# Transposing branch B's probabilities by DMA in 16-bit halves, with the attention steps at new slots

## The chip, the cores and the metric

The kernel runs on one core of one Trainium2 chip. Its time is what the device takes for one execution, in microseconds (us), and a version is timed in several runs, of which the median counts. The engines are named as in the profile: PE (TensorE, with PEld for its weight loads), DVE (VectorE), ACT (ScalarE), POOL (GpSimd) and SP (SyncE, which issues most DMA transfers). Each works through a queue of its own in order and meets the others only at semaphores.

## The reference

It is one decoder layer on 512 tokens of width 2048. One projection of the normed input feeds three token mixers; their outputs are gated, projected, weighted and summed. The change lies in branch B, the "forgetting attention" of 12 heads of width 64:

```python
def forgetting_attention(q, k, v, f_logit, q_gain, k_gain):
    ...
    c = jnp.cumsum(log_f, axis=1).transpose(0, 2, 1)
    ...
        sc = jnp.einsum('bqhd,bshd->bhqs', qb, k) * scale + cqb[..., None] - c[:, :, None, :]
        qpos = n * BLOCK + jnp.arange(BLOCK)
        mask = key_pos[None, :] <= qpos[:, None]
        sc = jnp.where(mask[None, None], sc, NEG)
        p = jax.nn.softmax(sc, axis=-1)
        return jnp.einsum('bhqs,bshd->bqhd', p, v)
```

Branch A is a sliding-window attention, also of 12 heads, and branch C a cross-attention of 4 heads into 256 memory tokens. All of it is float32.

## The kernel before

**Matmuls.** A float32 operand is split into a high and a low part (tensors with `h`/`hi` and `l`/`lo`, or weight tiles `wb` and `wc`), and each product is made of three matmuls. The weights come as a stream of units (`Stream`): a unit is 256 rows of one projection, four banks by two row blocks by three matmuls, 24 in all, each 128x384 or wider. For each unit SP fetches a raw tile `wa` (two buffers), ACT casts it to the high part `wb` in two casts (L212), and DVE subtracts for the low part `wc` (L215). When unit i begins, the casts of unit i+1 are recorded and the fetch of unit i+2.

**Slots.** The order of the work is fixed while the program is written down. A clock counts slots: three projection matmuls are half a slot, so a unit is four slots. `at_slot` and `later` put a step at a slot, and the tables at the top of the file say how far a step stands from its base. PE, DVE, ACT and POOL execute exactly in the order of recording; for SP's queue a scheduler chooses the order. Attention is thus woven into the projections: branch B's first six heads (0 to 5) run beside the projections of the second half of branch B, heads 6 to 11 beside those of branch A, branch A's heads beside the next, and so on. Slots are counted in this text from the first unit; branch B's attention stands between slots 96 and 288.

**One head of branch B** (`head_B`) is a chain of steps, and a step waits in the chain when a resource such as a PSUM bank ("T") or a buffer is not free in the program. `sb` makes a bias tile on POOL. `s1(i)`, for the four query blocks i, multiplies queries and keys (PE, tile `sB`), adds the bias and takes the maximum (DVE, L600), and later exponentiates (ACT, L603) and divides (DVE, L580 and L581), leaving the probabilities in `p` (`pB`), one row per query. `s2` transposes them on PE against an identity into PSUM (`ptB`, L625), ten blocks of 128x128 in three groups, and `split` casts each group to the high part `phB` (ACT, L556) and subtracts for the low part `plB` (DVE, L558). `s3` multiplies both with V (`avB`, L635, eight matmuls), and `pv_out` copies half of the result (`avsB`) and adds.

`prep` stands ahead of every second head: four transposes each of the queries (`tqB`) and of the keys (`tkB`), from which ACT makes two query copies (L538) and four key copies (L549, L552) and DVE the low parts (L539, L550).

A later stage of the kernel already has a transpose by DMA: `flip_dma` separates the two 16-bit halves of float32 values on ACT, sends them through `dma_start_transpose` in tiles of 128 partitions by 2048 halves, and ACT joins the halves again (L1478).

Of the kernel before, what the change touches and what calls it, by code (L numbers as in the profile page):

```python
# [20 lines left out]
P = 128  # L21
# [10 lines left out]
UK = 2  # L32
BOFF = (0, 512, 1024, 896)

BASES_B = ((14, 24, 35.5, 46, 52, 70.5), (15, 24, 34.5, 47, 58, 72.5))
# [6 lines left out]
PREP_Q = ((-1.5, 22.0, 38.5), (2.5, 18.5, 45.5))  # L42
PREP_K = ((6.5, 28.0, 44), (7, 26.5, 53.5))
PREP_A = (6, 18.5, 39.0, 46, 66.0, 76.5)
PREP_KA = (6.0, 32.5, 47.5, 68.0)

NORMS = {'qB0': (24.5, 3, 2), 'kB0': (10.5, 4.5, 4.5), 'qB1': (3.5, 3, 1.0), 'kB1': (1.5, 7.0, 1), 'qA0': (6, 2.5, 3.5), 'qA1': (6.0, 3.0, 1.5), 'kA': (0.5, 3, 0.0), 'mk': (8.0, 4.0, 0.0), 'qC0': (0.5, 3, 0), 'qC1': (4.5, 2.5, 1.5)}


LOW_W, LOW_M, LOW_Q, LOW_K, LOW_P = ((1.0, 1), (0.5, 1.5), 1, 1, 0.5)  # L50
EXP_B, EXP_A, EXP_C, DIV_B, DIV_A, DIV_C = (1.0, 0.5, 1.0, 3, 3.5, 3.0)
PV_B, PV_A = ((1.0, 3.5), (0.5, 1))
SUMS_X = (1, 13, 23, 133, 112, 207, 190, 225)

# [3 lines left out]
def tile_hybrid_block(ctx, tc, xT, x, memT, mem, ng, mng, w_in, b_forget, gqa, gka, sinks, gqb, gkb, gqc, gkc,  # L58
# [10 lines left out]
    def f32(ap):  # L69
        return ap.bitcast(F32)  # L70
# [72 lines left out]
    def later(dt, f):  # L143
        at_slot(clock[0] + dt, f)
# [11 lines left out]
            heapq.heappop(agenda)[2]()  # L156

    chains, chain_end = [], [0.0]
    free = {"T": 2, "P": 2, "PT": 1, "Q": 3, "KH": 3, "KL": 2, "bias": 2, "cb": 2}

    def release(*names):
        for n in names:
# [225 lines left out]
        at_slot(t0 + 24, lambda: root(ss, mrstd, 2))  # L388


    def qk_tile(name, tag, n, bufs):
        return tokp.tile([P, NT, n], F32, tag=tag, bufs=bufs, name=name)

# [29 lines left out]
    def evac_qk(key, tag, n, hd, bufs, scale=rstd, nt=NT, after=None):  # L423

        nh = n // hd
        state = {}

        def f(b, pb, c0=0):
            if after is not None:
                after(b, pb)  # L430
            if b == 0:
                state["t"] = tokp.tile([P, nt, n], F32, tag=tag, bufs=bufs, name=f"t_{key}")
            t = state["t"]
            if scale is None:
                ac.copy(t[:, b, :], pb[:, c0:c0 + n])
            else:
                ac.activation(t[:, b, :], pb[:, c0:c0 + n], AF.Copy, scale=scale[:, b:b + 1])
# [81 lines left out]
    def tbank(name):  # L519
        return bank(0, name)  # L520
# [62 lines left out]
    def head_B(h, kv):  # L583
# [3 lines left out]
        def s1(i):  # L587
# [14 lines left out]
            release("bias")  # L602
            later(EXP_B, lambda: ac.activation(pi, pi, AF.Exp, bias=nm, scale=-1.0, accum_out=den[:, i:i + 1]))  # L603
            later(DIV_B, lambda: scaled(pi, den, i, ve))

        def sb(i):
            n = (i + 1) * P
# [3 lines left out]
                             fill=NEG, base=0, channel_multiplier=1)  # L611
            s["b", i] = bi

        def s2(g):
            p = s["p"]
            if g == 0:
                s["hi"] = at.p.tile([P, 1280], F32R, tag="PH", bufs=1, name=f"phB{h}")
                s["lo"] = at.p.tile([P, 1280], F32R, tag="PL", bufs=1, name=f"plB{h}")
            off = (0, 128, 384, 768)
            grp, o, n = (((0,), 0, 512), ((1, 3), 512, 512), ((2,), 1024, 256))[g]  # L620
            tb = tbank(f"ptB{h}_{grp[0]}")
            c = 0
            for j in grp:
                for i in range(j, NT):
                    pe.transpose(tb[:, c:c + P], p[:, off[i] + j * P:off[i] + (j + 1) * P], ident)  # L625
# [13 lines left out]
        def done():  # L639
# [2 lines left out]
        o = STEPS_B  # L642
        steps = [(o[2], ["bias"], lambda: sb(0)), (o[3], ["bias"], lambda: sb(1)), (o[4], ["P"], lambda: s1(0)),
                 (o[5], [], lambda: s1(1)), (o[6], ["bias"], lambda: sb(2)), (o[7], ["bias"], lambda: sb(3)),
                 (o[8], [], lambda: s1(2)), (o[9], [], lambda: (s1(3), done())),
                 (o[10], ["T", "PT"], lambda: s2(0)), (o[11], ["T"], lambda: s2(1)),
                 (o[12], ["T"], lambda: (s2(2), release("P"))), (o[13], ["T"], lambda: (s3(), release("PT")))]
        return steps

    slopes = np.exp2((np.float32(-8.0) * np.arange(1, 13, dtype=np.float32) / np.float32(12)).astype(np.float32)).astype(np.float32)  # L650
# [250 lines left out]
            else:  # L901
                later(1 + 0.5 * k, lambda k=k: part(k))

    ev_mk = evac_qk("mk", "tkC", 512, 128, 1, scale=mrstd, nt=2)
    mvs = {}

    def evac_m(b, pb):
        if b < 2:
            ev_mk(b, pb)
            return  # L910
        t = b - 2
        if t == 0:
            mvs["v"] = tokp.tile([P, 2, 2, 512], F32R, tag="VC", bufs=1, name="V_C")
        v = mvs["v"]
        ac.activation(v[:, 0, t, :], pb, AF.Copy, scale=mrstd[:, t:t + 1])
        ve.scalar_tensor_tensor(out=v[:, 1, t, :], in0=pb, scalar=mrstd[:, t:t + 1], in1=f32(v[:, 0, t, :]),
                                op0=ALU.mult, op1=ALU.subtract)
        if t == 1:
            toks["mv"] = (v[:, 0], v[:, 1])

    ev_c = [evac_qk(f"qC{i}", "tq", 256, 128, 2) for i in range(2)]

# [528 lines left out]
        later(5, lambda: pair(0))  # L1451
        later(9 if cg < 3 else 10.5, lambda: pair(1))

    def u16(ap):
        return ap.bitcast(U16)

    def flip_dma(cg, y, g):


# [155 lines left out]
```

## Time and profile before

| what | value |
|---|---|
| median of 3 runs | 1482.01 us (1481.52 to 1482.14) |
| span of the profiled execution | 1480.7 us |
| PE busy | 1473.2 us, 99% |
| DVE, ACT, POOL busy | 1092.5, 727.5, 185.3 us |
| moved by DMA | 279.50 MB, mean 189 GB/s |
| granted clock of PE | 0.9 or more of full speed in every fortieth of the span |

The span runs from the first to the last instruction of one profiled execution; that execution has no separate time of its own beside it, and the timed runs, of which 1481.52 us is the lowest, lie 0.8 to 1.4 us above it. Busy times of PE overlap, since its matmuls are pipelined: the distance from one start to the next says more than the mean duration. A group's row reads: line, engine, operation, output from inputs, shapes and count, then busy time and mean duration in ns, then the engine's idle time before it and what ended that.

### The profile page before, as it was taken

To read this page: it belongs to the slowest core of one execution; us is meant where nothing else is said; L and a number is where in the kernel's file an instruction comes from. 1 tells how busy PE (TensorE), PEld (TensorE's weight loads), DVE (VectorE), ACT (ScalarE), POOL (GpSimd) and SP (SyncE) were. 2 spreads that over 40 slices of the span, in tenths; PEclk is the share of its full clock that TensorE was granted. 3 is DMA by queue.
4 is the path that set the end of the run, shared out by engine and by line. 5 is a ranking of instruction groups with operands and counts; after the bars stand their busy time and mean duration, and the time that the engine had idled before them with its cause. 6 is when DMAs were issued, how large, how long until landed. Compare 5 with 4: busy or idle time off the path is not lost.

```text
span 1480.7 us, 20354 instructions
## 1 busy us (share of the span) xinstructions
PE 1473.2 (99%) x7193; PEld 1272.6 (86%) x7193; DVE 1092.5 (74%) x1886; ACT 727.5 (49%) x1212; POOL 185.3 (13%) x223
## 2 busy tenths in 40 slices
PE   9999999999999999999999999999999999999998
PEld 9999999998888888888888888888888888888887
DVE  6385875775678666578888888888887566589997
ACT  5545654664467664555444443435354344245442
POOL 0121430331324430000000000000000201110000
PEclk9999999999999999999999999999999999999999
DMA  8774235333444323476667676767676876676674
GB/s 290 222 213 130 76 93 164 84 113 111 130 137 151 92 79 108 149 261 231 207 213 224 214 241 206 241 211 230 201 236 213 279 222 205 220 246 223 243 286 153
DMA packets 135630, 279.50 MB, mean 189 GB/s; under 512 B 22492, under 2 KB 62044, under 8 KB 135528
## 3 DMA queue, kind: packets, MB, share of 16 engines
q1 hardware_dynamic: 130488, 261.68, 55.8%
q10 hardware_dynamic: 5040, 16.53, 3.3%
q8 instruction: 56, 0.92, 0.2%
q14 instruction: 46, 0.38, 0.1%
HBM read 244.58 MB, written 31.48 MB: 186 GB/s over the span
## 4 chain that ended last, share of the span: by engine, by line
PE 96%; ACT 1%; DVE 1%; DMA 1%; issue 0%; POOL 0%; DVEq 0%; ACTq 0%; POOLq 0%
PE P L1085 41%; PE z L301 11%; PE qA L301 5%; PE kB L301 5%; PE vB L301 5%; PE uB L1085 4%; PE uA L1085 4%; PE qB L301 4%; PE qC L301 3%; PE kvA L301 3%; PE uC L1085 3%; PE mem L301 1%; PE avB L635 1%; PE ptB L625 1%; PE avA L702 1%; PE sB L577 1%
## 5 line engine op out<-in xcount | busy, mean ns | idle before, releaser
L215 DVE TENSOR_TENSOR wc<-wa,wb 128x512 fp32r<-128x512 f32 (+2 forms) x252 | 148.8, 629 | 75.3 <-ACT wb L212 71.7
L212 ACT CAST wb<-wa 128x512 fp32r<-128x512 f32 (+2 forms) x252 | 130.5, 567 | 146.3 <-PE z L301 34.5
L1127 ACT CAST wa<-rawl 128x1024 fp32r<-128x1024 f32 x85 | 89.4, 1052 | 208.1 <-DVE rawl L1017 149.8
L1017 DVE TENSOR_TENSOR rawl<-rawl 128x512 f32<-128x512 f32 x256 | 176.9, 692 | 6.3 <-DMA rawl<-in_w_out_dram 1.9
L1130 DVE TENSOR_TENSOR wc<-rawl,wa 128x1024 fp32r<-128x1024 f32 x85 | 105.0, 1235 | 52.0 <-ACT wa L1127 50.3
L1130 DVE TENSOR_TENSOR we<-rawl,wd 128x512 fp32r<-128x512 f32 (+1 forms) x128 | 122.2, 954 | 4.5 <-ACT wd L1127 0.9
L1401 POOL TENSOR_TENSOR y<-y,gA 128x512 f32<-128x512 f32 x16 | 28.1, 1788 | 727.8 <-DVE gA L1399 727.8
L1127 ACT CAST wd<-rawl 128x512 fp32r<-128x512 f32 (+1 forms) x128 | 106.9, 835 | 23.8 <-DVE rawl L1017 20.1
L301 PE MATMUL z<-ah,wb 128*128 128x512 f32 x256 | 101.8, 398 | 0.0
L301 PE MATMUL z<-ah,wc 128*128 128x512 f32 x256 | 99.9, 390 | 0.0
L301 PE MATMUL z<-al,wb 128*128 128x512 f32 x256 | 99.8, 390 | 0.0
L1127 ACT CAST wb<-rawl 128x1024 fp32r<-128x1024 f32 x43 | 45.3, 1053 | 87.4 <-DVE rawl L1017 62.1
L1085 PE MATMUL P<-wd,xhx 128*128 128x512 f32 x192 | 74.8, 390 | 0.0
L1085 PE MATMUL P<-we,xhx 128*128 128x512 f32 x192 | 74.7, 389 | 0.0
L1085 PE MATMUL P<-wd,xlx 128*128 128x512 f32 x192 | 74.7, 389 | 0.0
L1130 DVE TENSOR_TENSOR wb<-rawl,wb 128x1024 fp32r<-128x1024 f32 x43 | 52.5, 1222 | 25.5 <-ACT wb L1127 25.3
L1014 DVE TENSOR_TENSOR R<-P,R 128x512 f32<-128x512 f32 (+1 forms) x90 | 57.1, 674 | 6.4 <-PE P L1085 5.8
L301 PEld LDWEIGHTS z<-ah,wc 128*128 128x128 f32 x256 | 48.0, 188 | 10.2
L301 PEld LDWEIGHTS z<-ah,wb 128*128 128x128 f32 x256 | 48.1, 188 | 9.3 <-DVE zA L939 0.3
L301 PEld LDWEIGHTS z<-al,wb 128*128 128x128 f32 x256 | 48.2, 188 | 9.0
L581 POOL TENSOR_SCALAR pA<-pA,denA 128x256 f32<-128x256 f32 (+1 forms) x48 | 45.0, 953 | 79.5 <-DVE denA L580 79.5
L1085 PE MATMUL P<-wa,xlx 128*128 128x512 f32 x128 | 49.8, 389 | 0.0
(410 smaller groups left out, 4184.8 us busy)
## 6 DMA issues: line engine op xcount, KB each, us to landing
rawl<-in_w_in_dram SPq DMA_DIRECT2D x144, 512.0 KB, 4.5
rawl<-in_w_out_dram SPq DMA_DIRECT2D x48, 512.0 KB, 4.8
wa<-in_w_in_dram SPq DMA_DIRECT2D x62, 384.0 KB, 3.5
wa<-in_w_in_dram SPq DMA_DIRECT2D x64, 256.0 KB, 3.1
rawl<-in_w_in_dram SPq DMA_DIRECT2D x48, 256.0 KB, 4.1
gates<-R ACTq DMA_DIRECT2D x24, 512.0 KB, 7.3
wa<-in_w_in_dram SPq DMA_DIRECT2D x16, 512.0 KB, 3.7
wa<-in_w_mem_dram SPq DMA_DIRECT2D x16, 512.0 KB, 3.7
```

The lines of the kernel that those rows point to most:

```text
L212: ac.copy(hi[:, :n], raw[:, i, :n])
L215: ve.tensor_sub(lo[:, :n], raw[:, i, :n], f32(hi[:, :n]))
L301: pe.matmul(pb, a, m, start=b in fresh, stop=last and not todo[b])
L577: pe.matmul(dst, q[:, qs], kl[:, ks], start=False, stop=True)
L581: engine.tensor_scalar(p, p, den[:, 4 + i:5 + i], None, op0=ALU.mult)
L625: pe.transpose(tb[:, c:c + P], p[:, off[i] + j * P:off[i] + (j + 1) * P], ident)
L1014: ve.tensor_tensor(out, a, b, op=ALU.add)
L1017: ve.tensor_tensor(out, a, b, op=ALU.subtract)
L1085: pe.matmul(*args, **kw)
L1127: ac.copy(hi[:, :k, :], src)
L1130: return lambda: ve.tensor_tensor(lo[:, :k, :], src, f32(hi[:, :k, :]), op=ALU.subtract)
L1401: po.tensor_tensor(y, y, g, op=ALU.add)
```

## The change

Branch B's ten transposes of a head on PE give way to a transpose by DMA, and the slots of many steps are different.

- `halves(i)`: POOL copies the low and high 16-bit halves of the divided probabilities from `p` into a tile `s1` in seven pieces per head (256 to 512 halves each; L633, L635).
- `send`: one `dma_start_transpose` on SP takes the 128x2560 halves to `s2` (L640).
- `join`: ACT interleaves the halves again, in two copies of 1280 halves each, into `t` (named `ptB`, L648), now in SBUF.
- `s2`: one cast of 1280 columns on ACT (`phB`, L656). `s2l`: one subtraction of 1280 columns on DVE (`plB`, L659), which reads both inputs from SBUF.
- Three one-buffer tiles (`spare`, X0 to X2) hold `s1`, `s2` and `t`; the memory branch's V and keys, which are needed later, use the same three.
- New values in the tables for branch B's bases and steps, its preparations, all norms, and the slots of the sums.

```diff
-STEPS_B = (-12, -8.5, -2, -1.5, 0, 1, 1.0, 1.5, 3.5, 5, 12, 11.5, 14, 15.5)
+STEPS_B = (-11.5, -5.0, -2.5, -1.5, 0, 1, 2.0, 0.0, 3.0, 1.5, 10.0, 15.0, 17.5, 19.0, 24, 4.5)
...
-EXP_B, EXP_A, EXP_C, DIV_B, DIV_A, DIV_C = (1.0, 0.5, 1.0, 3, 3.5, 3.0)
+EXP_B, EXP_A, EXP_C, DIV_B, DIV_A, DIV_C = (2.5, 0.5, 1.0, 3.5, 3.5, 3.0)
...
-    free = {"T": 2, "P": 2, "PT": 1, "Q": 3, "KH": 3, "KL": 2, "bias": 2, "cb": 2}
+    free = {"T": 2, "P": 2, "PT": 1, "Q": 3, "KH": 3, "KL": 2, "bias": 2, "cb": 2, "S1": 1, "S2": 1, "RW": 1}
...
+    def spare(n, name, dtype=F32, cols=1280):
+        return tokp.tile([P, 1280 * 4 // mybir.dt.size(dtype)], dtype, tag=f"X{n}", bufs=1, name=name)[:, :cols]
...
             later(DIV_B, lambda: scaled(pi, den, i, ve))
+            s["p", i] = pi
+            if i > 1:
+                later(DIV_B + 0.5, lambda: halves(i))
...
-        def s2(g):
-            p = s["p"]
...
-            grp, o, n = (((0,), 0, 512), ((1, 3), 512, 512), ((2,), 1024, 256))[g]
-            tb = tbank(f"ptB{h}_{grp[0]}")
-            c = 0
-            for j in grp:
-                for i in range(j, NT):
-                    pe.transpose(tb[:, c:c + P], p[:, off[i] + j * P:off[i] + (j + 1) * P], ident)
-                    c += P
-            split(s["hi"][:, o:o + n], s["lo"][:, o:o + n], tb[:, :n])
+        def halves(i):
+            if i == 0:
+                s["s1"] = spare(0, f"s1B{h}", U16, 2560).rearrange("p (e j n) -> p e j n", e=2, n=P)
+            src = u16(s["p", i]).rearrange("p (j n e) -> p e j n", n=P, e=2)
+            n = min(i + 1, 3)
+            for e in (slice(0, 2),) if i < 2 else (slice(0, 1), slice(1, 2)):
+                po.tensor_copy(s["s1"][:, e, i:i + 3 * n - 2:3, :], src[:, e, :n, :])
+            if i == 3:
+                po.tensor_copy(s["s1"][:, :, 7:8, :], src[:, :, 3:4, :])
+                release("P")
+
+        def send():
+            s["s2"] = spare(1, f"s2B{h}", U16, 2560)
+            sy.dma_start_transpose(out=s["s2"].rearrange("p (x n) -> p x n", n=P),
+                                   in_=s["s1"].rearrange("p e j n -> p (e j n)"))
+            release("S1")
+
+        def join(n):
+            if n == 0:
+                s["t"] = spare(2, f"ptB{h}")
+            c = slice(n * 640, n * 640 + 640)
+            ac.copy(u16(s["t"][:, c]).rearrange("p (n e) -> p e n", e=2),
+                    s["s2"].rearrange("p (e n) -> p e n", e=2)[:, :, c])
+            if n == 1:
+                release("S2")
+
+        def s2():
+            ...
+            ac.copy(s["hi"], s["t"])
+
+        def s2l():
+            ve.tensor_tensor(s["lo"], s["t"], f32(s["hi"]), op=ALU.subtract)
+            release("RW")
...
-                 (o[8], [], lambda: s1(2)), (o[9], [], lambda: (s1(3), done())),
-                 (o[10], ["T", "PT"], lambda: s2(0)), (o[11], ["T"], lambda: s2(1)),
-                 (o[12], ["T"], lambda: (s2(2), release("P"))), (o[13], ["T"], lambda: (s3(), release("PT")))]
+                 (o[8], [], lambda: s1(2)), (o[15], ["S1"], lambda: (halves(0), later(0.5, lambda: halves(1)))), (o[9], [], lambda: (s1(3), done())),
+                 (o[10], ["S2"], send), (o[11], ["RW"], lambda: (join(0), later(0.5, lambda: join(1)))), (o[12], ["PT"], s2), (o[13], [], s2l),
+                 (o[14], ["T"], lambda: (s3(), release("PT")))]
```

A step stands at its head's base plus its value; in the list `s1(3)` follows `halves(0)`, at 4.5, so the send at 10 stands 5.5 slots behind `s1(3)`, the joins at 15 and 15.5, the cast at 17.5, the subtraction at 19 and the product with V at 24.

On PE, before, this stands where head 1's transposes are, inside a unit of the second key projection (`kB1`):

```order
L301 MATMUL kB1_3_1699<-wb31_1611,al0_81 128x384
L625 MATMUL ptB1_0_1750<-ident_68,pB1_1529 128x128 x4
L625 MATMUL ptB1_1_1756<-ident_68,pB1_1529 128x128 x4
L301 MATMUL kB1_0_1696<-wb32_1690,ah1_74 128x384
L301 MATMUL kB1_0_1696<-wc32_1691,ah1_74 128x384
```

In the changed kernel, PE goes from head 1's last score, through two to three units, to its product with V, and nothing of head 1 stands between; here is the end of that way, at slot 140, where a score of head 3 and the key preparation of the third pair follow:

```order
L301 MATMUL kB1_3_1717<-wb33_1777,al2_83 128x384
L668 MATMUL avB1_1928<-phB1_1810,V_vB0_1195 128x512
L668 MATMUL avB1_1928<-plB1_1811,V_vB0_1195 128x512
...
L585 MATMUL sB3_3_1939<-kB011_1631,qB011_1451 128x512
L586 MATMUL sB3_3_1939<-kl1_1230,qB011_1451 128x512
L540 MATMUL tkB02_1943<-ident_68,t_kB0_777 128x128 x4
L301 MATMUL kB1_0_1714<-wb34_1847,ah3_76 128x384
```

The transposes are gone, and the product with V stands later behind the scores than it did.

On ACT, before, this stands around head 8's casts and the key copies of the third pair of the second half (`kB12`):

```order
L556 CAST phB8_3454<-ptB8_0_3456 128x512
L556 CAST phB8_3454<-ptB8_1_3462 128x512
L556 CAST phB8_3454<-ptB8_2_3491 128x256
L603 ACTIVATE pB9_3407,denB9_3408<-pB9_3407,denB9_3408 128x384
L212 CAST wb61_3507<-wa61_3435 128x384 x2
L603 ACTIVATE pB9_3407,denB9_3408<-pB9_3407,denB9_3408 128x512
L566 COPY avsB8_3537<-avB8_3516 64x512
L549 ACTIVATE kB120_3544<-tkB12_3539,g_kb_606 64x512
```

In the changed kernel it is this, from slot 240 to 244:

```order
L212 CAST wb60_3414<-wa60_3357 128x384 x2
L612 ACTIVATE pB9_3304,denB9_3305<-pB9_3304,denB9_3305 128x512
L648 COPY ptB8_3436<-s2B8_3363 128x2x640 x2
L547 ACTIVATE qB120_3458<-tqB12_3453,gs_qb_577 64x512
L547 ACTIVATE qB121_3460<-tqB12_3453,gs_qb_577 64x512
L558 ACTIVATE kB120_3467<-tkB12_3462,g_kb_606 64x512
L561 ACTIVATE kB120_3467<-tkB12_3462,g_kb_606 64x512
L558 ACTIVATE kB121_3470<-tkB12_3462,g_kb_606 64x512
L561 ACTIVATE kB121_3470<-tkB12_3462,g_kb_606 64x512
L656 CAST phB8_3487<-ptB8_3436 128x1280
L212 CAST wb61_3492<-wa61_3418 128x384 x2
```

The joins, the query and key copies and the wide cast now stand between two weight casts.

On SP, the weight fetches of that stretch follow each other before:

```order
L202 DMA wa59_3303<-in_w_in_dram 128x2x384
L202 DMA wa60_3355<-in_w_in_dram 128x2x384
L202 DMA wa61_3435<-in_w_in_dram 128x2x384
L202 DMA wa62_3511<-in_w_in_dram 128x2x384
L202 DMA wa63_3578<-in_w_in_dram 128x2x512
```

In the changed kernel they have transposes among them:

```order
L202 DMA wa60_3357<-in_w_in_dram 128x2x384
L640 DMA_TRANSPOSE s2B8_3363<-s1B8_3252 128x20x128
L202 DMA wa61_3418<-in_w_in_dram 128x2x384
L202 DMA wa62_3496<-in_w_in_dram 128x2x384
L640 DMA_TRANSPOSE s2B9_3490<-s1B9_3391 128x20x128
L202 DMA wa63_3550<-in_w_in_dram 128x2x512
```

Twelve transposes enter SP's queue, one for each head.

More of the change, by code (lines that the diff above doesn't have):

```diff
@@ L430, in f @@
                 after(b, pb)
-            if b == 0:
+            if b == 0 and tag is None:
+                state["t"] = spare(2, f"t_{key}", F32, nt * n).rearrange("p (t n) -> p t n", n=n)
+            elif b == 0:
                 state["t"] = tokp.tile([P, nt, n], F32, tag=tag, bufs=bufs, name=f"t_{key}")
@@ L912, in evac_m @@
         if t == 0:
[L913 to L916, printed above, removed]
+            mvs["v"] = [spare(i, f"V_C{i}", F32R, 1024).rearrange("p (t n) -> p t n", n=512) for i in range(2)]
+        vh, vl = mvs["v"]
+        ac.activation(vh[:, t, :], pb, AF.Copy, scale=mrstd[:, t:t + 1])
+        ve.scalar_tensor_tensor(out=vl[:, t, :], in0=pb, scalar=mrstd[:, t:t + 1], in1=f32(vh[:, t, :]),
                                 op0=ALU.mult, op1=ALU.subtract)
         if t == 1:
-            toks["mv"] = (v[:, 0], v[:, 1])
+            toks["mv"] = (vh, vl)
     ev_c = [evac_qk(f"qC{i}", "tq", 256, 128, 2) for i in range(2)]
```

26 lines of the change are left out of this document (12 added, 14 removed).

## The prediction

> **What bounds the kernel now.** I read the page's busy times first, then the waits of TensorE, then TensorE's timeline around one removed step, then ScalarE's timeline, and last the single rows that stand nearest to what is new.
>
> ```profile
> span 1480.7 us, 20354 instructions
> ...
> PE 1473.2 (99%) x7193; PEld 1272.6 (86%) x7193; DVE 1092.5 (74%) x1886; ACT 727.5 (49%) x1212; POOL 185.3 (13%) x223
> ```
>
> ```profile
> PE warm_up L1540 <- DVE wz L1537: 1.9, 1, 1.9
> PE ptA L688 <- DVE kl L550: 0.7, 1, 0.7
> PE kB L301 <- ACT t_qB L437: 0.2, 1, 0.2
> ```
>
> TensorE is busy 99% of the span, and the second fence is its whole list of waits: 2.8 us in 1480.7. The span is therefore the sum of what TensorE's queue holds. A TensorE instruction that goes is worth its place in that queue, and any new lateness of another engine counts only where it makes TensorE wait. Every step of branch B lies in the stage that this row covers, apart from the last two or three heads (columns: stretch, its length, busy time and count by engine, granted clock, DMA share, GB/s):
>
> ```profile
> 120.00:290.00 170.00, 169.80 (x1027) 166.72 (x1026) 118.17 (x304) 95.49 (x218) 49.32 (x78) 1.00 0.37 104
> ```
>
> There TensorE works 169.8 of 170 us at the full granted clock, VectorE 70%, ScalarE 56%, GpSimd 29%, and the DMA engines carry 37% of their time. So there is room for the moved work, on average; the question is the moments.
>
> **What is removed: 120 transposes.** TensorE's timeline (start, duration) around one head, and the group row (busy, mean ns):
>
> ```profile
> 139.13 0.33 PE L301 MATMUL qB<-wc,ah 128*128 128x384 f32 x1
> 139.30 0.34 PE L301 MATMUL qB<-wb,al 128*128 128x384 f32 x1
> 139.48 1.04 PE L625 MATMUL ptB<-ident,pB 128*128 128x128 f32 x8
> 140.27 0.42 PE L301 MATMUL qB<-wb,ah 128*128 128x384 f32 x1
> 140.53 0.34 PE L301 MATMUL qB<-wc,ah 128*128 128x384 f32 x1
> ...
> 142.62 0.34 PE L301 MATMUL qB<-wb,al 128*128 128x384 f32 x1
> 142.79 0.38 PE L625 MATMUL ptB<-ident,pB 128*128 128x128 f32 x2
> 142.93 0.42 PE L301 MATMUL qB<-wb,ah 128*128 128x384 f32 x1
> 143.19 0.34 PE L301 MATMUL qB<-wc,ah 128*128 128x384 f32 x1
> ...
> L625 PE MATMUL ptB<-ident,pB 128*128 128x128 f32 x120 | 17.0, 272 | 0.0
> ```
>
> Matmuls overlap, so I count from start to start. A projection matmul takes 0.174 us (139.13 to 139.30). Eight transposes take 139.48 to 140.27, 0.79 us, and the first matmul behind them 0.26 instead of 0.17: 0.88 us in all. Two more take 0.14 and the same 0.09 behind them: 0.23 us (the sum of the unrounded starts is 1.10 for both). Twelve heads make 12 x 1.10 = 13.2 us. The group's busy 17.0 us counts the overlap with the next matmul and is the upper end; 120 x 0.099 = 11.9 us, without the slower matmul behind, is the lower end. I take 13.2: in the new order nothing stands where the groups stood, and the scores, the products with V and the head preparations are as many as before. From the first step of branch A on, TensorE's order is the same.
>
> **What is added, by engine.** ScalarE loses three casts a head and gets two joins of 1280 halves and one cast of 1280. Its prices, again from start to start, are in its timeline and in two rows of the late stage that already joins halves:
>
> ```profile
> 143.56 0.93 ACT L212 CAST wb<-wa 128x384 fp32r<-128x384 f32 x2
> 144.40 0.61 ACT L603 ACTIVATE pB<-pB,denB 128x384 f32<-128x384 f32 x1
> ...
> 145.01 0.56 ACT L437 ACTIVATE t_qB<-qB,rstds 128x384 f32<-128x384 f32 x1
> 145.47 0.67 ACT L549 ACTIVATE kB<-tkB,g_kb 64x512 fp32r<-64x512 f32 x1
> ...
> 148.26 0.58 ACT L437 ACTIVATE t_qB<-qB,rstds 128x384 f32<-128x384 f32 x1
> 148.74 0.71 ACT L603 ACTIVATE pB<-pB,denB 128x512 f32<-128x512 f32 x1
> ...
> 149.57 0.58 ACT L566 COPY avsB<-avB 64x512 f32<-64x512 f32 x1
> ...
> 1201.19 1.39 ACT L1478 COPY y3s<-yh 128x512 uint16<-128x512 uint16 x2
> ...
> 1204.49 1.04 ACT L1002 CAST wa<-rawl 128x1024 fp32r<-128x1024 f32 x1
> ```
>
> A weight cast costs 0.42 (two in 0.84), the exponentials 0.61 and 0.83 with their read-out, the four key copies 2.79 together, 0.70 each, and a query copy, of the same size, as much. Two joins of 512 take 1.39, the second starting 0.63 after the first. For 1280 halves the bounds are 0.63 + 768 x 0.82 ns = 1.26 us, at a cast's rate, and 2.5 x 0.63 = 1.57; between them I take 1.42. The 1280-wide cast, from the 1024-wide one at 1.04, costs 1.2. The new 4.0 us a head replace about 1.3, so ScalarE gains 2.7 x 12 = 32 us of work in some 200 us: 56% becomes about 72%. This is hidden as long as the weight casts come in time. The cast for unit u+1 is issued when unit u begins, and unit u keeps TensorE 4 slots (24 matmuls, 4.2 us), so a cast may start about 3 us late.
>
> Two places use that up. They need TensorE's other steps:
>
> ```profile
> 144.07 0.40 PE L576 MATMUL sB<-kB,qB 128*128 128x512 f32 x1
> ...
> 144.54 0.60 PE L531 MATMUL tkB<-ident,t_kB 128*128 128x128 f32 x4
> ...
> 145.51 0.40 PE L635 MATMUL avB<-phB,V_vB 128*128 128x512 f32 x1
> ...
> 146.75 0.39 PE L301 MATMUL qB<-wb,ah 128*128 128x384 f32 x1
> ...
> L215 DVE TENSOR_TENSOR wc<-wa,wb 128x384 fp32r<-128x384 f32 x68 | 36.2, 573 | 7.0 <-ACT wb L212 6.8
> ```
>
> Head 8, slots 241.5 to 248: ScalarE's queue holds the two joins (2.84), two query copies (1.40), four key copies (2.79), the wide cast (1.2) and only then the cast of wb61 (0.42), with about 0.2 left of an exponential ahead: 8.85 us, and VectorE's low half 0.57 more, 9.4. TensorE reaches the matmul that needs it after 39 matmuls (6.8), two groups of four transposes (0.44 each) and one small score (0.25): 7.9 us. It waits 1.5. In the order before, wb61's cast stands ahead of the key copies.
>
> Head 2, slots 140 to 148: product with V (1.24), score (0.47) and key transposes (0.44) come first, 2.2 us, and 48 matmuls (8.35): 10.5. ScalarE can begin its key copies only after those 2.2 us; then 2.79, two casts 0.84, 0.61, 0.58, 0.83, two joins with a square between them 3.25, and wb36's cast 0.42: 11.5, and 0.57 more: 12.1. TensorE waits 1.6. Together I charge 3.1 us; elsewhere the same count leaves at least 0.4 us (a square is taken at a cast's price, having its width). The bounds are 0 (ScalarE gets ahead, no wait) and, with joins of 1.57, two more of 0.15 at each place, 3.7.
>
> GpSimd gets seven copies a head; these are the nearest rows, with the first of them reading a scalar per partition and computing, the second the slowest of its kind:
>
> ```profile
> L609 POOL TENSOR_SCALAR biB<-cb,cq 128x384 f32<-128x384 f32 x12 | 9.3, 772 | 90.8 <-DVE denB L600 90.8
> ...
> L581 POOL TENSOR_SCALAR pA<-pA,denA 128x256 f32<-128x256 f32 x36 | 34.4, 970 | 0.0
> ...
> L581 DVE TENSOR_SCALAR pB<-pB,denB x48: 286/421/640, 127.1 to 345.6; 128x128 f32<-128x128 f32 x12, 128x256 f32<-128x256 f32 x12, 128x384 f32<-128x384 f32 x12, 128x512 f32<-128x512 f32 x12
> ```
>
> The price of a 384-element piece lies between 0.77 and 1.45 (970 ns times 1.5). I take 0.77, since it runs in the same stage; the last three pieces then take 2.1 us.
>
> The transfer has a near row too, four transposes of 2048 columns (SP's issue time min/median/max, then the landing), beside the weight fetches of this stage:
>
> ```profile
> L1469 SPq DMA_TRANSPOSE yh<-gC x4: 1637/2816/3939, 1191.7 to 1238.0; - x4
> ...
> DMA to landing us min/median/max: 3.8/4.9/6.0
> ...
> wa<-in_w_in_dram SPq DMA_DIRECT2D x30, 384.0 KB, 3.3
> ```
>
> For 2560 columns that is 4.8, 6.1 or 7.5 us. From a head's last score the exponential comes 2.5 slots later (2.6 us at 1.04 a slot, 3.2 with the attention steps between), then 0.83, a division of about 0.65 and the copies 2.1: 6.8 us. With 6.1 the data are there after 12.9 us, and the first join stands 10.5 slots behind the score, 11 to 13.4 us. So the joins wait between nothing and 1.5 us, which the 3 us of a weight cast cover away from the two places; I charge 0.5 us for all. SP's queue holds the weight fetches behind the transpose, at worst 3.9 x 1.25 = 4.9 us; they are issued a unit ahead (4.2 us, landing in 3.3) and the cast has its own 3 us, so nothing is charged. VectorE's one subtraction of 1280 replaces three with the same elements. The product with V stands 19.5 slots, over 20 us, behind the last score, and the chain through both joins, cast and subtraction needs about 12.9 + 2.9 + 1.2 + 1.5 = 18.5: covered. The tables move the norms as well; the last ones still end ahead of the transposes that read them, charged at zero.
>
> Sum: -13.2 + 3.1 + 0.5 = -9.6 us on the profiled 1480.7, that is 1471.1. The runs' median 1482.0 is 1.3 above that span, so 1472.4.
>
> **Rivals.** (a) No wait at all: ScalarE, being free between, meets both places in time. TensorE's clean wait list speaks for it, the two counts against. 1482.0 - 13.2 = 1468.8.
>
> (b) Late joins: GpSimd's pieces cost the pA row's rate, 1.45, so the last three take about 3.9 us, and VectorE's divisions, which show 640 ns instead of 286 beside GpSimd, wait for them too. The joins come 2 to 2.5 us late at most heads, ScalarE stands still meanwhile with weight casts behind, and about four places beside the two lose 1 to 1.5 us: some 5 us more, 1477.5. For it: GpSimd's rows scatter widely; against: the stage's own row is the cheaper.
> By the Trainium skill (SBUF — State Buffer, Who interferes with whom) a VectorE instruction with two SBUF inputs and a GpSimd instruction that reads SBUF shut each other out for a whole instruction. The low-half subtraction read one input from PSUM before and reads both from SBUF now, so by that rule it joins the weight subtractions as a blocker of the seven copies; the sum would then be (b)'s.
>
> (c) Slower: the transposes hold up the weight fetches. SP stands at the transpose until GpSimd has finished, then issues for up to 4.9 us, and the fetch behind lands last. If that made TensorE wait at every head, it pays above 13.2 / 12 = 1.1 us a head; at 2 us it ends at 1482.0 - 13.2 + 24 = 1492.8. It needs a fetch over 4 us later than now, against a DMA share of 0.37.
>
> **How the numbers follow.** The forecast, 1472.4, holds about 0.5, (a) 0.15, (b) 0.25, (c) 0.10, three quarters of it beyond no change. A measurement of this kernel can tell about 0.2%, 3 us. Faster (under 1479): 0.5 + 0.15 + 0.25 = 0.90; same 0.03; slower 0.07. The range from (a) to (b), with the joins' upper bound inside, is 1468 to 1478.5 and leaves out (c) and a little of either end.
>
> **What would show it.** No ptB on TensorE; its list of waits has one at wb61 and one at wb36 of 1 to 2 us and little else; joins of 1.3 to 1.6 us; the stretch from the first score of head 0 to the first step of branch A about 10 us shorter, everything behind it unchanged. Wrong would be: waits of TensorE at most heads (b or c), joins that wait long for the transpose, GpSimd pieces above 1 us, or a difference in the later stages.

## The result: 1471.2 us, 0.7% faster

The median of five runs is 1471.16 us (1470.12 to 1471.67), against 1482.01 us before: a ratio of 0.9925 with a 95% interval of 0.9913 to 0.9937. The forecast was 1472.4, so the total is 1.2 us off; not every term under it was as close.

The page of the changed kernel:

```profile
span 1469.3 us, 20218 instructions
...
PE 1460.2 (99%) x7073; PEld 1261.3 (86%) x7073; DVE 1095.3 (75%) x1862; ACT 759.0 (52%) x1212; POOL 245.6 (17%) x307
```

The span is 11.4 us shorter, TensorE has 120 instructions less, ScalarE 31.5 us and GpSimd 60.3 us more work. TensorE is still the bound, but its list of waits, all of it, is longer than before:

```profile
PE warm_up L1570 <- DVE wz L1567: 1.9, 1, 1.9
PE sB L586 <- DVE kl L559: 1.3, 1, 1.3
PE kB L301 <- DVE wc L215: 0.8, 2, 0.6
PE qB L301 <- DVE wb L339: 0.3, 1, 0.3
PE kB L301 <- ACT wb L212: 0.2, 1, 0.2
PE qA L301 <- DVE wc L215: 0.2, 1, 0.2
```

To see where the time went I take two projection matmuls that both kernels have, the first of slot 96 and the first of slot 288, in TensorE's timeline before:

```profile
109.27 0.33 PE L301 MATMUL qB<-wb,ah 128*128 128x384 f32 x1
...
370.06 0.39 PE L301 MATMUL z<-ah,wb 128*128 128x512 f32 x1
```

and after:

```profile
108.59 0.33 PE L301 MATMUL qB<-wb,ah 128*128 128x384 f32 x1
...
360.65 0.39 PE L301 MATMUL z<-ah,wb 128*128 128x512 f32 x1
```

Between them branch B's attention runs: 260.79 us before, 252.06 after. This length, "the stage" from here on, lost 8.73 us. Another 0.68 us was gained ahead of it, where the first projection matmuls of this execution took 0.32 us each, instead of 0.17, up to 6.1 us and not up to 7.9, and 2.0 us behind it. The stage holds the same matmuls in both kernels, apart from the 120 transposes. So of the 13.2 us that the transposes took, about 4.5 us came back inside the stage.

**Where they came back.** TensorE's timeline after, at head 8's place (slots 241.5 to 248) and the units behind it:

```profile
296.75 0.22 PE L585 MATMUL sB<-kB,qB 128*128 128x128 f32 x1
298.23 0.33 PE L586 MATMUL sB<-kl,qB 128*128 128x128 f32 x1 [1.26 <-DVE kl L559]
...
298.79 0.34 PE L301 MATMUL qA<-wb,al 128*128 128x384 f32 x1
299.14 0.44 PE L301 MATMUL qA<-wb,ah 128*128 128x384 f32 x1
299.74 0.63 PE L301 MATMUL qA<-wc,ah 128*128 128x384 f32 x1 [0.15 <-DVE wc L215]
...
302.19 0.52 PE L301 MATMUL qA<-wc,ah 128*128 128x384 f32 x1
302.51 0.52 PE L301 MATMUL qA<-wb,al 128*128 128x384 f32 x1
```

Counted from start to start, the score with the key's low half `kl` comes about 1.4 us late, the first matmuls with wb61 and wc61 0.18 and 0.42. From there to 303.15 a projection matmul takes 0.32 us (302.19 to 302.51) instead of 0.174: some 1.4 us more. And at head 2's place:

```profile
169.01 0.34 PE L301 MATMUL kB<-wb,ah 128*128 128x384 f32 x1
169.99 0.44 PE L301 MATMUL kB<-wc,ah 128*128 128x384 f32 x1 [0.64 <-DVE wc L215]
...
173.92 0.34 PE L301 MATMUL kB<-wb,al 128*128 128x384 f32 x1
174.44 0.44 PE L301 MATMUL kB<-wb,ah 128*128 128x384 f32 x1 [0.18 <-ACT wb L212]
175.03 0.45 PE L301 MATMUL kB<-wc,ah 128*128 128x384 f32 x1 [0.15 <-DVE wc L215]
```

Here 0.81 us is lost at wc35 (0.98 instead of 0.17), then 0.35 and 0.42 at wb36 and wc36. Together that is 5.0 us, where the kernel before has 0.4 us of such losses: a net 4.6, the missing time within 0.1.

The wait at wc35 is not the joins' doing: head 2's first join starts at 170.45, behind it. VectorE stands until ScalarE's key copies end, makes two key low halves, and only then the weight's low part:

```profile
167.83 1.51 DVE L559 SCALAR_TENSOR_TENSOR kl<-tkB,g_kb,kB 64x512 fp32r<-64x512 f32 x2 [1.44 <-ACT kB L561]
169.37 1.03 DVE L215 TENSOR_TENSOR wc<-wa,wb 128x384 fp32r<-128x384 f32 x2
```

What ScalarE did ahead of head 8's waits, and VectorE behind it (`kl` is here the low half of the keys of heads 10 and 11, which TensorE needs for head 10's first score):

```profile
290.01 3.16 ACT L648 COPY ptB<-s2B 128x1280 uint16<-128x1280 uint16 x2
293.20 1.38 ACT L547 ACTIVATE qB<-tqB,gs_qb 64x512 fp32r<-64x512 f32 x2
294.60 0.69 ACT L558 ACTIVATE kB<-tkB,g_kb 64x512 fp32r<-64x512 f32 x1
...
296.71 0.69 ACT L561 ACTIVATE kB<-tkB,g_kb 64x512 fp32r<-64x512 f32 x1
297.42 1.26 ACT L656 CAST phB<-ptB 128x1280 fp32r<-128x1280 f32 x1
298.58 0.92 ACT L212 CAST wb<-wa 128x384 fp32r<-128x384 f32 x2
```

```profile
297.43 1.53 DVE L559 SCALAR_TENSOR_TENSOR kl<-tkB,g_kb,kB 64x512 fp32r<-64x512 f32 x2 [1.28 <-ACT kB L561]
```

ScalarE works without a gap from the joins to wb61's cast. VectorE stands 1.28 us until the key copies end at 297.40, and only then makes `kl`, for which TensorE stands. The queue is the one the prediction counted; the first to be late in it is the key's low half and not wb61.

**Prices.** What the profile gives for the tiles `ptB`, `s1B` and `s2B` (ns, min/median/max; the last row, of `s2B`, is from issue to landing in us):

```profile
L648 ACT COPY ptB<-s2B x24: 1635/1651/1672, 133.5 to 342.6; 128x1280 uint16<-128x1280 uint16 x24
L656 ACT CAST phB<-ptB x12: 1252/1258/1279, 138.7 to 345.2; 128x1280 fp32r<-128x1280 f32 x12
L659 DVE TENSOR_TENSOR plB<-ptB,phB x12: 1473/1485/1811, 140.4 to 347.2; 128x1280 fp32r<-128x1280 f32 x12
...
  DMA s2B<-s1B: 4.7, 3
```

```profile
L633 POOL COPY s1B<-pB x72: 393/510/1769, 123.1 to 335.6; 128x384 uint16<-128x384 uint16 x48, 128x256 uint16<-128x256 uint16 x12, 128x512 uint16<-128x512 uint16 x12
```

```profile
L640 SPq DMA_TRANSPOSE s2B<-s1B x12: 2412/2564/2706, 128.7 to 337.0; - x12
...
DMA to landing us min/median/max: 4.1/4.2/5.4
```

The joins wait for the transfer three times in 24, 4.7 us in all. The stretch that the prediction quoted, after; its busy times (PE, PEld, DVE, ACT, POOL) and then clock, DMA share and GB/s:

```profile
120.00:290.00 170.00, 169.03 (x992) 166.25 (x991) 121.84 (x302) 120.39 (x229) 96.45 (x148) 1.00 0.54 142
299.00:303.00 4.00, 3.83 (x13) 3.45 (x13) 3.36 (x7) 2.45 (x6) 2.09 (x1) 0.60 0.43 114
```

ScalarE is at 71% (72% was forecast) and GpSimd at 57%. The second row is the stretch of slow matmuls: a granted clock of 0.60 on average.

### The profile page after: what moved, and what is told of

It is laid out like the page before. It is cut to its first block, busy times and chain, and to the rows that moved or that the text cites. A ratio compares the mean times of both kernels' runs of the same rounds, so it can differ in the third digit from the quotient of the medians.

```text
span 1469.3 us, 20218 instructions
## 1 busy us (share of the span) xinstructions
PE 1460.2 (99%) x7073; PEld 1261.3 (86%) x7073; DVE 1095.3 (75%) x1862; ACT 759.0 (52%) x1212; POOL 245.6 (17%) x307
## 4 chain that ended last, share of the span: by engine, by line
PE 97%; ACT 2%; POOL 1%; DVE 0%; issue 0%; DMA 0%; SPq 0%; DVEq 0%; POOLq 0%; ACTq 0%
PE P L1118 41%; PE z L301 12%; PE qB L301 5%; PE vB L301 5%; PE uB L1118 4%; PE uA L1118 4%; PE kB L301 4%; PE mem L301 3%; PE qC L301 3%; PE kvA L301 3%; PE uC L1118 3%; PE qA L301 3%; PE avB L668 1%; PE avA L735 1%; ACT ptB L648 1%; PE sB L586 0%
## 5 line engine op out<-in xcount | busy, mean ns | idle before, releaser
L1118 PE MATMUL P<-wa,xhx 128*128 128x512 f32 x128 | 49.8, 389 | 0.0
```

Source lines behind the costliest of these rows:

```text
L1118: pe.matmul(*args, **kw)
```

## Experiments

Two theories ran against each other. The first: ScalarE's longer work at the two crowded places makes TensorE wait there, and these places can be relieved. The second: without the transposes TensorE comes earlier to engines that were just in time, so a third of the gain comes back as waits wherever slack is shortest, and a place relieved hands the wait on. The lengths of the stage, measured between the same two matmuls in each profiled execution, with the medians (us):

| kernel | stage | against before | median |
|---|---|---|---|
| before | 260.8 | | 1482.0 |
| changed | 252.1 | -8.7 | 1471.2 |
| e1: before, transposes left out | 252.3 | -8.5 | 1473.3 |
| e2: before, with the new slots of one norm | 260.8 | 0.0 | 1482.2 |
| e3: changed, with the old slots of that norm | 250.8 | -10.0 | 1471.2 |
| e4: two places relieved | 251.3 | -9.5 | 1470.7 |
| e5: transposes back on TensorE, early | 278.4 | +17.6 | 1499.1 |
| e6: one join only | 247.9 | -12.9 | 1467.9 |
| e7: transposing left out | 252.3 | -8.5 | 1472.1 |
| e8: transfer issued twice | 284.5 | +23.7 | 1505.9 |
| e9: idle transposes on TensorE | 262.6 | +1.8 | 1483.1 |
| e10: pieces copied twice | 267.6 | +6.8 | 1487.0 |
| e11: second join on GpSimd | 250.5 | -10.3 | 1470.2 |
| e12: that, and the order mended | 249.8 | -11.0 | 1469.1 |

One profiled execution of a kernel can differ from the next here: the kernel of e3, whose work in the stage is that of the changed kernel, had 250.8, with the same wait at `kl` and without the slow clock behind it. Its losses from start to start at the same places are 3.6 us, where the changed kernel's execution has 5.0. Differences of 1 us in the stage prove nothing by themselves.

### e1: the kernel before without its transposes

```diff
...
-                    pe.transpose(tb[:, c:c + P], p[:, off[i] + j * P:off[i] + (j + 1) * P], ident)
...
+            src = p[:, o:o + n]
...
```

> The kernel before, with its ten transposes per head on PE left out: the casts and subtractions read the untransposed probabilities from SBUF at the same slots. Theory (a transpose is worth its place in PE's queue): 12 x 1.10 = 13.2 us less than before, 1468.8, bounds 11.9 and 17.0 us less. Rival (part of the transposes lay in time that PE would have lost anyway): less than 10 us, above 1472.

1473.31 us, a ratio of 0.9942 (0.9929 to 0.9956). Even where no engine gets new work and no slot moves, taking 13.2 us off TensorE yields only 8.5 in the stage; the median lies above the 1472 that the rival gave as its least. The largest entry on TensorE's list is new:

```profile
PE avB L634 <- DVE plB L558: 2.8, 4, 0.8
```

The product with V, which had the transposes between itself and the score, now comes to the low half too early. This speaks for the second theory, with another wait than in the changed kernel.

### e2 and e3: the memory branch's norm at the other's slots

Of the 2.0 us behind the stage 1.5 lie at slots 336 to 352, which made me suspect the moved norm of the memory keys (`mk`). e2 is the kernel before with its new slots, e3 the changed kernel with the old ones:

```diff
-'mk': (8.0, 4.0, 0.0)
+'mk': (1.0, 11.5, 6.5)
```

> The kernel before, with one entry of its tables changed to the new value: the slots of the memory keys' norm, (8, 4, 0) to (1, 11.5, 6.5). Theory (1.45 us of the gain come from the memory projection, where PE waited for a crowded DVE at the head of branch A that this norm crowds): 1.4 us less, 1480.6, and PE's wait of 0.7 us at ptA is gone from its list. Rival (the difference there is one execution's chance): 1482.0 within 0.4, the wait stays.

> The changed kernel, with the memory keys' norm at its old slots (8, 4, 0). Theory: 1.4 us more than the changed kernel, 1472.6, and a wait of PE at ptA of about 0.7 us comes back. Rival (chance of one execution): 1471.2, no such wait.

1482.17 us (ratio 1.0000, 0.9991 to 1.0009) and 1471.17 us (0.9928, 0.9915 to 0.9942): the norm's slots do nothing for the time, and this theory fell. The time from slot 288 to the end is shorter in every kernel that reaches slot 288 at another moment than before, whether 13 us earlier or 24 us later, by 0.4 to 2.4 us. What sets it stays open.

### e4: the two crowded places relieved

```diff
-PREP_Q = ((0.0, 15.5, 41.0), (-1.5, 27.5, 50.5))
+PREP_Q = ((0.0, 15.5, 41.0), (-1.5, 27.5, 48.5))
...
+        if h == 2:
+            o[11] += 1.5
+            o[12] += 0.5
+        if h == 8:
+            o[12] += 0.5
```

> The changed kernel with ScalarE's two crowded places spread out and nothing else: head 2's joins 1.5 slots later and its cast half a slot later, head 8's cast half a slot later, and the query preparation of the third pair of the second half 2 slots earlier. Theory (PE's remaining waits in branch B come from ScalarE's queue at these two places): the excess of 1.6 us at head 2 and of 3.4 us at head 8, half clock included, goes: 1466.2, granted clock 1.00 throughout branch B. Rival (they come from late crossbar transfers or late GpSimd pieces, wherever the joins stand): within 1 us of 1471.2, the waits move but stay.

1470.69 us (ratio 0.9924, 0.9911 to 0.9936), hardly different from the changed kernel: the rival's number, though not its cause, as e7 will show. The stage is 0.5 us longer than in e3's execution. The waits at wb36, wb61 and `kl` are gone; their time turned up elsewhere:

```profile
PE tkB L540 <- DVE ysB L579: 1.0, 1, 1.0
PE kvA L301 <- ACT t_qA L446: 0.7, 2, 0.5
```

So moving work between slots moves the wait, as the second theory says.

### e5 and e9: the transposes back on TensorE

e5 gives the changed kernel its old transposes again, with unused results, 4 slots behind the last score. e9 does it with the identity as input, at the slot of the transfer:

```diff
+            for grp in ((0,), (1, 3), (2,)):
+                tb, c = sbank(f"unused{h}_{grp[0]}"), 0
+                for j in grp:
+                    for k in range(j, NT):
+                        pe.transpose(tb[:, c:c + P], ident, ident)
+                        c += P
```

> The changed kernel with ten transposes per head put back on TensorE, their results unused; everything on the other engines stays as in the changed kernel. Theory (the other engines were just in time, and once the transposes are gone TensorE outruns them, which hands back 4 to 5 us as waits): with the 13.2 us back in TensorE's queue most of the new waits close again, so the time rises by 8 to 10 us only, to about 1480, and the waits at wb36, wc35, the key low half of pair 3 and wb61 shrink to under 1 us together. Rival (the waits are set by ScalarE's queue at its crowded places, whatever TensorE does): they stay, and the time rises by the whole 13.2 us, to 1484.4.

> The changed kernel with ten transposes per head put back on TensorE at the slot of the DMA transpose, but of the identity instead of the probabilities, so that they wait for no division; their results are unused. (With the probabilities, 4 slots behind the last score, they waited 11.3 us for VectorE, which spoiled the comparison.) Theory (TensorE, relieved of 13.2 us, outruns engines that were just in time, and 4 to 5 us come back as waits): with the time back in TensorE's queue the waits at wb36, wc35, the low half of pair 3's key and wb61 close, and the time rises by 8 to 9.5 us, to 1479 to 1480.7. Rival (ScalarE's crowded places cost their waits whatever TensorE does): 1484.4.

e5 took 1499.11 us and tells nothing on the question: so early the probabilities aren't divided yet, and TensorE stood 11.3 us for them. e9 took 1483.08 us, a ratio of 1.0007 (0.9998 to 1.0017) to the kernel before, 11.9 us above the changed kernel: between the two expectations, and nearer to the rival's 1484.4. What is left of its waits besides the warm-up is short:

```profile
PE kB L301 <- DVE wc L215: 0.7, 1, 0.7
PE sB L586 <- DVE kl L559: 0.5, 1, 0.5
```

From start to start 2.1 us of the 5.0 remain: 0.8 at wc35, 0.7 at `kl`, 0.6 at wb61 and wc61. The transposes lengthen the stage by 10.6, and 2.9 us of losses close: 13.5 us, near the 13.2 that the prediction counted for the transposes. But 1.4 of these 2.9 us are the slow stretch, which e3's execution lacks as well. Against that one the stage is 11.8 us longer, as the medians say too, and of 3.6 us of losses 1.5 close. TensorE's lead over the others thus makes less than half of the waits; the rest stays when TensorE has its time back.

### e6: one join instead of two

```diff
...
-            ac.copy(s["hi"], s["t"])
+            ac.copy(s["hi"].rearrange("p (a n) -> p a n", a=2), s["t"][:, :640].unsqueeze(1).to_broadcast([P, 2, 640]))
...
-                 (o[10], ["S2"], send), (o[11], ["RW"], lambda: (join(0), later(0.5, lambda: join(1)))), (o[12], ["PT"], s2), (o[13], [], s2l),
+                 (o[10], ["S2"], send), (o[11], ["RW"], lambda: join(0)), (o[12], ["PT"], s2), (o[13], [], s2l),
```

> The changed kernel with only the first of a head's two joins; the wide cast and the subtraction read its half twice. It leaves half of the joining out. ScalarE loses 12 x 1.5 us. Theory of crowded places (ScalarE's queue in front of wb36 and wb61 is what TensorE waits for): both places lose the 1.5 us that their waits need, the waits there vanish with the half-clock stretch behind, and 3 to 4 us come back: 1467 to 1468. Rival (the lateness moves on: VectorE's low halves and the PSUM banks are next, as when only the two places were given other slots, 1470.7): 1469.5 to 1471.

This kernel leaves the second half of the probabilities unjoined and uses the first in its place. 1467.87 us, a ratio of 0.9905 (0.9888 to 0.9921), and the stage 12.9 us shorter than before: nearly all of the 13.2. The waits at `kl` and wb36 are gone; besides the warm-up TensorE's longest entry is now the 0.6 us at wc35.

The first theory is right after all in what it names: ScalarE's work is what costs, except at wc35. Where e4 only moved work within ScalarE's queue and the wait went along, e6 removes 1.5 us a head, and the wait doesn't come back. The second theory has a share: TensorE got faster than ScalarE's queue by more than that queue had to spare. But 13 us more on TensorE (e9) leave 2.1 us of losses from start to start, 18 us less on ScalarE (e6) only 1.2: 0.8 at wc35 and 0.4 at wc61.

### e7 and e8: the transfer

e7 leaves the transposing out: the joins read GpSimd's halves directly, from two tiles in turn (first part); e8 issues each transpose by DMA twice (second part).

```diff
...
-            sy.dma_start_transpose(out=s["s2"].rearrange("p (x n) -> p x n", n=P),
-                                   in_=s["s1"].rearrange("p e j n -> p (e j n)"))
+            s["s2"] = s["s1"].rearrange("p e j n -> p (e j n)")
...
```

```diff
+            sy.dma_start_transpose(out=s["s2"].rearrange("p (x n) -> p x n", n=P),
+                                   in_=s["s1"].rearrange("p e j n -> p (e j n)"))
```

> The changed kernel without the transpose by DMA: the joins read GpSimd's halves directly, in the same order on every engine but SP. It leaves the transposing out. It shows what the transfer's lateness and its place on SP cost. Theory: the joins waited 4.7 us for the transfers in sum, under the cover of the weight casts' 3 us, so 0 to 0.7 us come back: 1470.5 to 1471.2. Rival (the transfers, on SP's queue and beside the weight fetches, cause part of the lost 4.6 us): 2 us or more come back, under 1469.2.

> The changed kernel with each transposing DMA issued twice in a row on SP. The second adds about 2.6 us of issue on SP and 4 us to the landing, 7.9 MB more are moved. Theory: the joins come 2.5 to 4 us later at most heads, which is beyond the 3 us that a weight cast may be late at the crowded places; they wait over 25 us in sum and TensorE loses 3 to 8 us: 1474 to 1479. Rival (a transfer's lateness is hidden up to several us, since the cast behind has its own slack): within 0.7 us of the changed kernel.

e7: 1472.13 us (ratio 0.9935, 0.9920 to 0.9950), with a wait of 1.5 us at `kl` and the slow clock behind it. The transfer costs nothing. e8: 1505.89 us (1.0162, 1.0147 to 1.0178), far outside both expectations. The waits of ScalarE and GpSimd for the transfers, and two of TensorE's rows:

```profile
ACT ptB L650 <- DMA s2B<-s1B: 54.5, 11, 7.5
POOL s1B L633 <- DMA s2B<-s1B: 22.7, 5, 7.1
```

```profile
PE vB L301 <- ACT wb L212: 6.2, 2, 6.1
PE sB L585 <- ACT kB L561: 4.9, 1, 4.9
```

The second transpose starts about 4.2 us behind the first, when that one has landed, and lands 4.8 us later, so the data come some 4.7 us later than the usual 4.2. The joins wait 50 us more, and the stage is 32 us longer. GpSimd's pieces, which need the tile that the transfers read, wait 22.7 us instead of 1.1, so not all of the 32 need come by way of the joins. The second transposes also hold up SP, but ScalarE's weight casts stand only 0.3 us in the stage for a fetch. The transfer is free where it stands, but 4.7 us of room it has not; how much it has wasn't tried.

### e10: GpSimd's pieces copied twice

```diff
-                po.tensor_copy(s["s1"][:, e, i:i + 3 * n - 2:3, :], src[:, e, :n, :])
+                for _ in range(2):
+                    po.tensor_copy(s["s1"][:, e, i:i + 3 * n - 2:3, :], src[:, e, :n, :])
```

> The changed kernel with GpSimd copying each piece of the first kind twice: six more copies a head, 0.5 us each by the changed kernel's rows, of which three or four lie behind the last division. Theory: the transfers start 1.5 to 2 us later, the joins wait some 20 us in sum instead of 4.7, and TensorE loses 1 to 5 us: 1472 to 1476. Rival (GpSimd's work, with the wait for it on SP, has 2 us of room in front of the transfer): within 0.7 us of the changed kernel. If GpSimd's reading held VectorE off for whole instructions, VectorE's waits would also grow at places without a join, and the time would go above 1478.

1486.97 us, a ratio of 1.0034 (1.0021 to 1.0047): 15.8 us above the changed kernel, well over what theory and rival gave. The joins wait 27.9 us, for some 20 expected; a second way shows in the engines' timelines around 300 us (GpSimd, then VectorE, then TensorE):

```profile
296.81 2.09 POOL L634 COPY s1B<-pB 128x384 uint16<-128x384 uint16 x4
...
299.89 0.29 POOL L622 TENSOR_SCALAR_AFFINE_SELECT biB<-biB 128x128 f32<-128x128 f32 x1
```

```profile
300.22 0.56 DVE L609 CUSTOM_DVE_ANT_0 pB<-sB,biB 128x384 f32<-128x384 f32 x1 [5.04 <-POOL biB L622]
```

```profile
303.62 0.66 PE L540 MATMUL tkB<-ident,t_kB 128*128 128x128 f32 x2 [2.73 <-DVE ysB L579]
```

The pieces of one head stand on GpSimd ahead of the next head's bias tile. VectorE waits 5.04 us for that tile, with the sum that releases a PSUM bank behind it, and TensorE 2.73 us for the bank. VectorE's waits for bias tiles are 21 us here and 4 us in the changed kernel. The time lies above 1478 us, where the third expectation put instructions held off for their whole length. But a VectorE instruction that is held off shows as a longer one (the 1.91 us row under e11), and VectorE's busy time hardly rose (1099.0 us against 1095.3): the waits are for work that stands behind other work on GpSimd.

### e11 and e12: a better split

```diff
-            ac.copy(u16(s["t"][:, c]).rearrange("p (n e) -> p e n", e=2),
+            (ac.copy if n == 0 else po.tensor_copy)(u16(s["t"][:, c]).rearrange("p (n e) -> p e n", e=2),
```

> The changed kernel with the second of the two joins of every head on GpSimd instead of ScalarE. Theory (ScalarE's queue is what is crowded, as the run with one join showed by 3.3 us): GpSimd takes 1.7 us for it (2.5 pieces of 512 at about 0.67), beside the first join, and most of the 3.3 us comes back: 1468 to 1469.5. Rival (GpSimd's queue, now standing at the transfer, delays the next head's bias tiles and pieces): no gain, 1471 to 1474.

1470.17 us (ratio 0.9919, 0.9904 to 0.9934). The wait at `kl` is gone, and 1.0 us of the median comes back, where 1.7 to 3.2 were expected; against e3's execution the stage is shorter by 0.3 us only. One of the new waits is at a weight of `kvA` (1.1 us); GpSimd's and VectorE's timelines just ahead of it:

```profile
339.52 1.62 POOL L648 COPY ptB<-s2B 128x1280 uint16<-128x1280 uint16 x1
```

```profile
339.60 1.91 DVE L422 TENSOR_TENSOR t_qA<-t_qA,nr_qA 128x384 f32<-128x384 f32 x1 [1.44 <-POOL nr_qA L382]
```

The same multiplication takes 0.56 us elsewhere; this one begins beside GpSimd's join and outlasts it. By the Trainium skill (SBUF — State Buffer, Who interferes with whom) a VectorE instruction with two SBUF inputs and a GpSimd instruction that reads SBUF exclude each other for a whole instruction, and this pair of rows agrees with it.

e12 leaves heads 9 to 11 as they were and lets wc35's subtraction go ahead of the two key low halves:

```diff
-        later(LOW_K, lambda: ve.scalar_tensor_tensor(out=kl[0:64, :], in0=tb[r, :], scalar=g[r, :], in1=f32(kh[0:64, :]),
+        later(LOW_K + (0.5 if name[:4] == "kB02" else 0), lambda: ve.scalar_tensor_tensor(out=kl[0:64, :], in0=tb[r, :], scalar=g[r, :], in1=f32(kh[0:64, :]),
...
-            ac.copy(u16(s["t"][:, c]).rearrange("p (n e) -> p e n", e=2),
+            (ac.copy if n == 0 or h > 8 else po.tensor_copy)(u16(s["t"][:, c]).rearrange("p (n e) -> p e n", e=2),
...
```

> The second join on GpSimd for heads 0 to 8 (heads 9 to 11 as in the changed kernel), and at slot 144 the subtraction of wc35 on VectorE ahead of the two key low halves instead of behind them. Of the 2.8 us that TensorE lost in the stage with the second join on GpSimd for all heads, 0.8 stood at wc35 and 1.25 at a wc of kvA, where VectorE's multiplication took 1.91 us beside GpSimd's join of head 10 or 11 instead of 0.56. Theory: both go, and nothing stands behind them: 1470.2 - 2.0 = 1468.2. Rival (the wait moves to the next place, as it did when the two crowded places were relieved): 1469.5 to 1470.5.

1469.09 us, a ratio of 0.9916 (0.9902 to 0.9930): the lowest median of those kernels that leave nothing out, 2.1 us below the changed kernel, or 1.3 by the two ratios, with intervals that overlap. It lies between theory and rival, and the trace shows what the rival said: the wait at wc35 went, and the next unit's took its place:

```profile
PE kB L301 <- DVE wc L215: 1.2, 1, 1.2
```

## Why the prediction was right

**The transposes, -13.2 us: right.** e6 keeps 12.9 of them, and e9, which puts as many back, accounts for 13.3 to 13.5. The start-to-start count, neither the group's busy 17.0 nor 11.9, was the proper measure.

**ScalarE's places, +3.1 us: right places, the cause right in the main, too small.** They cost 5.0 us in this execution and 3.6 in e3's. Head 8 was to cost 1.5 at wb61; it cost about 3.4, 1.4 at the key's low half, 0.6 at wb61 and wc61, and 1.4 by the slow clock behind, which e3 hasn't. The step that failed is the count up to wb61: it followed ScalarE's queue to the weight cast and passed over the key copies in the same queue, whose low halves TensorE needs for head 10's first score, ahead of wb61's matmuls. Head 2 was to cost 1.6 at wb36; it cost 0.77 there and 0.81 one unit earlier, at wc35, where VectorE's queue has the key low halves ahead of the weight. The sum fits by luck: the wait at wc35 comes ahead of the joins, and stays in e6 and e9.

**Late joins, +0.5 us: none.** GpSimd's pieces of 384 took 0.51 us at the median (0.77 was taken), the transfer landed after 4.2 us (6.1). Both margins were better than forecast, and e7 shows that the transfer costs nothing. Five pieces of 84 took over 1 us, which was to be a sign of (b): the wide subtraction does shut them out, as the prediction feared (last section), but no wait of TensorE follows close on one. e10 and e8 show that lateness would have cost more than (b) or (c) says, each by another way: in e10 the bias tiles behind the pieces, which (b) missed, and in e8 the joins and GpSimd's pieces. The late weight fetches, (c)'s mechanism, no run shows.

**Joins 1.42 us:** 1.5 from start to start (3.16 for two, less 1.65), inside the bounds of 1.26 and 1.57; the wide cast 1.16 for 1.2.

**"Everything behind it unchanged": wrong,** by 2.0 us of gain, and 0.7 ahead. The stage was forecast at -9.6 and gave -8.7 (-10.0 in e3); the gains outside it outweighed the error, and a larger distance between span and median (1.9 us, forecast 1.3) took part of that back. Runs of either kernel whose own span is known lie 1.7 to 1.9 us above it, so the 1.3 set a median beside the span of an execution that was somewhat longer than usual. That the total is closer than its parts is luck.

**Rival (a), no wait at all,** is nearly what e6 reaches, at 1467.9 with 1.2 us of losses left, and only with 18 us less on ScalarE.

## What to carry to other kernels

Work taken off the bounding engine is worth its start-to-start time less what the next queue lacks; find that lack by following, behind each added instruction of an in-order engine, every tile that the bounding engine will ask for, in its own order, and not only the one you suspect. Here moving the work to other slots passed the wait on (e4), shortening the crowded queue removed it (e6), and giving part of it to GpSimd removed that wait and brought smaller ones elsewhere (e11, e12). Before trusting that a transfer is hidden, double it: here a hidden one turned into 32 us when it came 4.7 us later and held its tile for longer.

## What the chip showed that was not expected

- **A slow clock after a short wait.** Behind the 1.26 us wait at 296.75 TensorE ran for 3.4 us at about half speed, which cost as much again as the wait. e7 has such a stretch behind its wait of 1.5 us; the wait of 1.3 us in e3 had nothing of the kind behind it. The Trainium skill (TensorE: Matmul & The Clock Gate, Part 1) puts the fall to half clock behind an idle window of about 3.4 us that runs freely; the length of the slow stretch fits, but the idle time here was far shorter, so an idle window of that length was not needed for it. What decides between e3 and the others stays open.
- **A transpose by DMA of 655 KB** (128 x 2560 halves) lands 4.1 to 5.4 us after its issue, median 4.2, though the four smaller ones of 2048 columns in the late stage took 3.8 to 6.0, median 4.9.
- **GpSimd's 16-bit pieces** go from 0.39 to 1.77 us. The five over 1 us all begin while a VectorE instruction with two SBUF inputs runs (four times the wide subtraction, once a weight's) and end 0.26 to 0.37 us behind it; for one of them, which takes 0.40 us at the median of its shape, GpSimd's row and VectorE's:

```profile
184.62 1.59 POOL L633 COPY s1B<-pB 128x256 uint16<-128x256 uint16 x1 [0.90 <-DVE pB L590]
184.47 1.49 DVE L659 TENSOR_TENSOR plB<-ptB,phB 128x1280 fp32r<-128x1280 f32 x1
```

It is e11's pair the other way round: here VectorE began first and GpSimd waited.
